# A two-layer decoder trunk on one core: early memsets and first fills on VectorE, routing tables made in two steps, the overflow path written as loops

## The chip, the core and the metric

The kernel runs on one core of a Trainium2 chip. Its time is what the device reports for one execution, in microseconds (us); of several runs the median is taken. PE is TensorE, DVE VectorE, ACT ScalarE, POOL GpSimd, and SP the engine that only issues transfers and waits. Each engine runs its own instructions in order; semaphores tie them together.

## What is computed

A sequence of 256 tokens of width 1024 passes two layers. Each sub-layer is `x + gate * fn(rms_norm(x) * (1 + scale) + shift)`, where shift, scale and gate come from the conditioning vector `c` by a 1024 x 3072 product:

```python
def ada_params(c, w, b):
    mod = jax.nn.silu(c) @ w + b
    shift, scale, gate = jnp.split(mod, 3, axis=-1)
...
    for i in range(DEPTH):
...
        x = modulated_residual(x, c, norm_g[i, 0], mod_w[i, 0], mod_b[i, 0], mixer)
        x = modulated_residual(x, c, norm_g[i, 1], mod_w[i, 1], mod_b[i, 1], channel)
    return rms_norm(x, final_g)
```

Layer 0 has a short gated convolution and a dense SwiGLU, layer 1 dilated attention and eight SwiGLU experts, of which each token takes two.

All weights are float32 in HBM, some 395 MB; every one of them is read once.

## The kernel before, in words

**The weight stream.** One object, `Stream`, holds all weight loads in the order of use. SP issues them (L279 for split weights, L305, L343 and L354 for the modulation weights, L480 for the experts) into a ring of buffers of 1 MB. A load is issued when its buffer is free. Each transfer counts on one of eight semaphores in turn, so SP also waits until the transfer eight places earlier has landed. For the dense layers a weight is split into two rounded halves: ACT writes `whi` (L218), DVE the rest `wlo` (L220), and PE multiplies three times (`hTh` by `whi`, `hTl` by `whi`, `hTh` by `wlo`).

**The start.** The first modulation (`Mod` 0) is summed on PE: `cb`, silu of `c` spread over 32 columns, times the raw weights, into `tp`. DVE adds the sums to the bias rows in `macc` (L317), PE spreads the rows with the selector tiles `pick`, and DVE multiplies with the norm weights `gb` (L374). `macc` is cleared by POOL before SP may issue the transfers of its bias rows; in SP's program these stand behind the first two weight loads and ahead of all others:

```python
            self.acc = pool.tile([P, 512], F32, name="macc", bufs=2)
            self.summed = False
            gp.memset(self.acc, 0.0)
            for n, c0 in enumerate(cols):
                dma.dma_start(self.acc[64 * n:64 * n + 1], self.b[c0:c0 + 512].rearrange("(o n) -> o n", o=1))
```

`gb` is one row copied to all partitions by POOL's `partition_broadcast`; `dif`, the table behind the identity `ident`, is a POOL `iota`.

**The dense feed-forward stage** takes 22 weight units, one after the other. `hooks` hangs other work behind units by their number; `make_routing` hangs behind unit 0. It makes the experts' tables: POOL iotas `part`, `slotc`, `tri`, `slot`, and nine DVE operations on them. In DVE's order it stands ahead of `hTl` of the second half of the features, which unit 2 is the first to need.

**The experts** run one after another, 34.6 MB of weights each. Ahead of expert 1 every engine that takes part reads the flag `over` from SBUF, which says whether an expert has over 128 tokens, and branches (L1514, L1515). With these inputs none has, so `overflow()` is not run. PE's first product of expert 1 waits for DVE to have passed that If.

Of the kernel before, what the change touches and what calls it, by code (L numbers as in the profile page):

```python
# [22 lines left out]
KT = D // P  # L23
FF = 2816
NE = 8
# [4 lines left out]
EPS = 1e-6  # L30
# [22 lines left out]
def trunk_kernel(ctx: ExitStack, tc: tile.TileContext, a, out):  # L53
    nc = tc.nc
    ve, sc, pe, gp = nc.vector, nc.scalar, nc.tensor, nc.gpsimd

    cst = ctx.enter_context(tc.tile_pool(name="cst", bufs=1))
    pers = ctx.enter_context(tc.tile_pool(name="pers", bufs=1))
# [4 lines left out]
    def f32(ap):  # L63
        return ap.bitcast(F32)
# [16 lines left out]
    x = pers.tile([P, NT, D], F32, name="x")  # L81
# [23 lines left out]

    pick = [early.tile([P, P], F32, name=f"pick{n}") for n in range(2)]
    for n in range(2):
        gp.memset(pick[n], 0.0)
        for r in (64 * n, 64 * n + 32):
            gp.memset(pick[n][r:r + 1], 1.0)  # L110
    warm = cst.tile([P, 1], F32, name="warm")
    sc.activation(warm, eps, AF.Sqrt)

# [29 lines left out]
    class Stream:  # L143
# [143 lines left out]
    class Mod:  # L287
# [5 lines left out]
        def start_pe(self, pool, cols, dma=gp):  # L293


            self.acc = pool.tile([P, 512], F32, name="macc", bufs=2)
# [89 lines left out]
    mods = [Mod(s) for s in range(4)]  # L386
# [293 lines left out]
    rw = cst.tile([P, KT, NE], F32, name="rw")  # L680
# [6 lines left out]
    slotc = cst.tile([P, 7], F32, name="slotc")  # L687
    slot = None

    def make_routing():  # L690
        nonlocal slot

        part = cst.tile([P, 7], I32, name="part")
        gp.iota(part, pattern=[[0, 7]], base=0, channel_multiplier=1)
        partf = cst.tile([P, 7], F32, name="partf")
        for c, n, m, base, step in ((0, 1, 63, 1, 0), (1, 2, 31, 65, 32), (3, 4, 31, 1, 32)):
            c = slice(c, c + n)
            ve.tensor_scalar(part[:, c], part[:, c], m, None, op0=OP.bitwise_and)
            gp.iota(slotc[:, c], pattern=[[step, n]], base=base, channel_multiplier=0, allow_small_or_imprecise_dtypes=True)
        ve.tensor_copy(partf, part)  # L700
        ve.tensor_add(slotc, slotc, partf)
        nc.sync.dma_start(rw, a["router_w"][0].rearrange("(k p) e -> p k e", p=P))
        gp.iota(tri, pattern=[[1, NE], [-1, NE]], base=0, channel_multiplier=0, allow_small_or_imprecise_dtypes=True)
# [551 lines left out]
    def overflow():  # L1255

        wg, wu, wd = a["moe_w_gate"][0], a["moe_w_up"][0], a["moe_w_down"][0]
        ov = moe.tile([P, FF], F32, name="ov", tag="acts")
        hs = ov[:, 2048:2560]
        wts = deque(pers.tile([P, 512], F32, name="ovw", tag="rtmp", bufs=3) for _ in range(2))  # L1260
        gov = moe.tile([P, NT, NE], F32, name="gov")
        po, pg = sums_of
        for i in range(NT):
            ve.scalar_tensor_tensor(gov[:, i], px[:, i], P + 0.5, gates[:, i], op0=OP.is_gt, op1=OP.mult)
        for i in range(NT):
            hTo = ov[:, :D].rearrange("p (k t) -> p k t", t=P)
            for q in range(2):
                c = slice(q * 512, q * 512 + 512)
                ve.tensor_add(hs, f32(hh[:, i, c]), f32(hl[:, i, c]))
                p = turn_tile().rearrange("p (k t) -> p k t", k=4)  # L1270
                for k in range(4):
                    pe.transpose(p[:, k], hs[:, k * P:(k + 1) * P], ident)
                sc.activation(hTo[:, 4 * q:4 * q + 4], p, AF.Copy)
            for e in range(NE):
                for f0 in range(0, FF, 256):
                    for n, w in enumerate((wg, wu)):
                        for k in range(0, KT, 2):
                            wts.rotate()
                            wt = wts[0].rearrange("p (k n) -> p k n", k=2)
                            gp.dma_start(wt, w[e, k * P:(k + 2) * P, f0:f0 + 256].rearrange("(k p) n -> p k n", p=P))  # L1280
                            for kk in range(2):
                                mm(pg[:, n * 512:n * 512 + 256], hTo[:, k + kk], wt[:, kk], k + kk == 0, k + kk == KT - 1)
                    sg = ov[:, D:D + 256]
                    sc.activation(sg, pg[:, :256], AF.Silu)
                    ve.tensor_mul(sg, sg, pg[:, 512:768])
# [3 lines left out]
                    sT = ov[:, D + 256:D + 512].rearrange("p (f t) -> p f t", t=P)  # L1289
                    sc.activation(sT.rearrange("p f t -> p (f t)"), p[:, :256], AF.Copy)  # L1290
                    for f in range(2):
                        r0 = f0 + f * P
                        for h in range(2):
                            wts.rotate()
                            wt = wts[0]
                            gp.dma_start(wt, wd[e, r0:r0 + P, h * 512:h * 512 + 512])
                            mm(po[:, h * 512:h * 512 + 512], sT[:, f], wt, r0 == 0, r0 + P == FF)
                for h in range(2):
                    c = slice(h * 512, h * 512 + 512)
                    og = ov[:, D + 512:D + 1024]  # L1300
                    ve.tensor_mul(og, po[:, c], mods[3].G[:, c])
                    ve.scalar_tensor_tensor(x[:, i, c], og, gov[:, i, e:e + 1], x[:, i, c], op0=OP.mult, op1=OP.add)

    hh = hl = None
    rs, nxt, lps = {}, {}, {}
# [199 lines left out]
                ve.scalar_tensor_tensor(x[:, i, cs], ps[i][c], gates[:, i, e:e + 1], x[:, i, cs], op0=OP.mult, op1=OP.add)  # L1505

    _, n_all = nc.values_load_multi_w_load_instructions(counts[0:1, :], engines=[mybir.EngineType.PE], min_val=0, max_val=S)
    engines = [mybir.EngineType.PE, mybir.EngineType.Activation, mybir.EngineType.DVE, mybir.EngineType.Pool]
    tc.mark_branch_hint_location("overflow", "LikelyTaken", engines)
    for e in range(NE):  # L1510
        pr, b = divmod(e, 2)
        n_before, n_of = n_of, n_all[e]
        if e == 1:
            flag = nc.values_load(over[0:1, 0:1], engines=engines, min_val=0, max_val=1)  # L1514
            with tc.If(flag > 0, label="overflow"):  # L1515
                overflow()
        if e == NE - 2:
            fg = pers.tile([P, D], F32, name="fg", tag="gb")
# [138 lines left out]
```

## Time and profile before

| | us |
|---|---|
| median of 3 runs | 1209.56 (1209.32 to 1211.14) |
| the profiled execution | 1213.32 |
| its span | 1211.5 |
| PE busy | 1106.7 (91%) |
| DVE busy | 548.5 (45%) |
| ACT busy | 320.7 (26%) |
| POOL busy | 32.1 (3%) |
| read from HBM | 395.45 MB, 327 GB/s over the span |

The stages by the clock of the trace: the convolution layer to about 150 us, the dense feed-forward layer to 380, attention to 490, the experts to the end. PE's busy share is an average over stages in which different things end last, so it says little about an edit in one of them. The stretch and the wait around each edit have to be read.

### The profile page before, as it was taken

The numbers are of one execution on the slowest core, as the hardware profiler recorded it, in microseconds if no ns is written. First come the engines' busy times: TensorE is split into PE (matmuls) and PEld (weight loads), VectorE is DVE, ScalarE is ACT, GpSimd is POOL, SyncE is SP. The second block draws the span as 40 slices with busy tenths as digits, with TensorE's granted clock in tenths as the row PEclk, the third lists the DMA queues.
The fourth block names the chain that finished last, engine by engine and source line by source line (L and its number), as shares of the span: only waits on it lengthen the run. The fifth ranks groups of instructions, "written<-read, shape, count | busy, mean of one in ns | idle before, by whom it ended". The sixth has DMA issues, their size and how long they took to land. (4 is left out here: it accounts for less than half of the span.)

```text
span 1211.5 us, 20568 instructions
## 1 busy us (share of the span) xinstructions
PE 1106.7 (91%) x8658; PEld 614.3 (51%) x8658; DVE 548.5 (45%) x853; ACT 320.7 (26%) x517; POOL 32.1 (3%) x56
## 2 busy tenths in 40 slices
PE   3999979999999999897999999999999999998985
PEld 0799679998878877432323333333333333322233
DVE  1599778897869966431222121211221222222123
ACT  2244434444344573321111110110010011110111
POOL 3010110000001000000000000000000000000000
PEclk9899989999999999998999999999999999999998
DMA  6898768787847835799999999999779999999993
GB/s 241 312 351 315 234 236 296 276 288 300 295 168 261 287 140 208 301 404 407 406 405 407 404 406 408 377 361 400 290 281 404 404 374 408 405 406 408 404 367 109
DMA packets 139401, 398.41 MB, mean 329 GB/s; under 512 B 11299, under 2 KB 22331, under 8 KB 139274
## 3 DMA queue, kind: packets, MB, share of 16 engines
q1 hardware_dynamic: 138698, 396.47, 86.1%
q8 instruction: 101, 1.65, 0.6%
q14 instruction: 26, 0.21, 0.0%
q0 software_dynamic: 576, 0.07, 0.0%
HBM read 395.45 MB, written 1.05 MB: 327 GB/s over the span
## 5 line engine op out<-in xcount | busy, mean ns | idle before, releaser
L73 PE MATMUL mm<-raw,xg 128*32 128x512 f32 (+1 forms) x1616 | 242.5, 566 | 21.4 <-DVEq L1515 7.6
L73 PE MATMUL mm<-rawr,xg 128*32 128x512 f32 (+1 forms) x1360 | 167.7, 559 | 7.7 <-PEq L1417 4.2
L220 DVE TENSOR_TENSOR wlo<-raw,whi 128x1024 fp32r<-128x1024 f32 (+2 forms) x130 | 154.0, 1222 | 30.8 <-ACT whi L218 30.0
L218 ACT ACTIVATE whi<-raw 128x1024 fp32r<-128x1024 f32 (+2 forms) x130 | 132.2, 1045 | 125.7 <-PE mm L73 90.7
L1424 DVE TENSOR_TENSOR gu<-gu,mm 64x512 f32<-64x512 f32 (+1 forms) x96 | 62.0, 646 | 217.7 <-ACT gu L1423 217.3
L73 PE MATMUL mm<-hTl,whi 128*128 128x256 f32 x544 | 148.8, 287 | 8.0 <-DVE hTl L531 8.0
L73 PE MATMUL mm<-hTh,whi 128*128 128x256 f32 x544 | 151.4, 293 | 1.4 <-ACT hTh L530 1.4
L73 PE MATMUL mm<-hTh,wlo 128*128 128x256 f32 x544 | 147.9, 285 | 0.8 <-DVE wlo L220 0.8
L73 PEld LDWEIGHTS mm<-raw,xg 128*32 128x32 f32 x1616 | 70.0, 111 | 131.8 <-issue 112.7
L1423 ACT ACTIVATE gu<-mm 64x512 f32<-64x512 f32 (+1 forms) x96 | 51.5, 552 | 304.6 <-PE mm L73 190.7
L73 PEld LDWEIGHTS mm<-hTl,whi 128*128 128x128 f32 x544 | 102.7, 195 | 11.3 <-DVE hTl L531 8.2
L73 PEld LDWEIGHTS mm<-hTh,whi 128*128 128x128 f32 x544 | 103.9, 198 | 3.9 <-ACT hTh L530 2.1
L73 PEld LDWEIGHTS mm<-rawr,xg 128*32 128x32 f32 x1360 | 51.1, 109 | 103.3 <-issue 89.3
L73 PEld LDWEIGHTS mm<-hTh,wlo 128*128 128x128 f32 x544 | 102.5, 194 | 1.0 <-DVE wlo L220 1.0
L73 PE MATMUL mm<-raw,acts 128*32 128x512 f32 (+1 forms) x784 | 87.8, 566 | 12.7 <-DMA raw<-in_moe_w_down_dram 6.9
L73 PE MATMUL mm<-rawr,acts 128*32 128x512 f32 x608 | 73.7, 595 | 4.4 <-PEq L1415 1.6
L1435 DVE COPY acts<-tp 128x256 f32<-128x256 f32 (+1 forms) x48 | 19.2, 401 | 92.5 <-ACT acts L1243 92.3
L73 PEld LDWEIGHTS mm<-raw,acts 128*32 128x32 f32 x784 | 26.4, 110 | 67.1 <-issue 53.6
L285 DVE SCALAR_TENSOR_TENSOR acc_ab<-raw,csil,acc_ab 128x1024 f32<-128x1024 f32 x40 | 51.2, 1281 | 6.4 <-DMA acc_ab<-in_mod_b_dram 5.7
L73 PE MATMUL mm<-whi,hTh 128*128 128x512 f32 (+1 forms) x128 | 50.1, 409 | 0.8 <-ACT hTh L530 0.7
L73 PE MATMUL mm<-rawx,xg 128*32 128x512 f32 (+1 forms) x224 | 47.9, 560 | 2.1 <-DMA rawx<-in_moe_w_up_dram 1.5
L1481 DVE TENSOR_TENSOR og<-mm,G 128x512 f32<-128x512 f32 x14 | 9.0, 686 | 89.4 <-PEq L1417 51.8
(267 smaller groups left out, 1331.2 us busy)
## 6 DMA issues: line engine op xcount, KB each, us to landing
raw<-in_moe_w_down_dram SPq DMA_DIRECT2D x36, 1024.0 KB, 13.1
rawr<-in_moe_w_down_dram SPq DMA_DIRECT2D x66, 512.0 KB, 10.0
raw<-in_mod_w_dram SPq DMA_DIRECT2D x64, 512.0 KB, 5.1
raw<-in_moe_w_gate_dram SPq DMA_DIRECT2D x29, 1024.0 KB, 14.0
raw<-in_moe_w_up_dram SPq DMA_DIRECT2D x27, 1024.0 KB, 12.1
rawr<-in_moe_w_up_dram SPq DMA_DIRECT2D x48, 512.0 KB, 10.2
rawr<-in_moe_w_gate_dram SPq DMA_DIRECT2D x48, 512.0 KB, 10.5
raw<-in_mod_w_dram SPq DMA_DIRECT2D x16, 1024.0 KB, 5.9
```

What stands on the lines that cost most here:

```text
L73: pe.matmul(o, l, r, start=start, stop=stop, skip_group_check=True)
L218: sc.activation(hi[:n, :c1 - c0], src, AF.Copy)
L220: ve.tensor_sub(lo_, src, f32(hi)))
L285: ve.scalar_tensor_tensor(acc, w, csil[:, k:k + 1], acc, op0=OP.mult, op1=OP.add)
L1423: sc.activation(a[64:, :N], bank[g][:64, :N], AF.Silu)
L1424: ve.tensor_mul(a[64 * g:64 * g + 64, :N], a[64:, :N], bank[g][64:, :N])
L1435: copy(acts[:, 8 * r:8 * r + 2 * nb, g:g + 32].rearrange("p (j m) t -> p m j t", j=2), v[:, :, n])
L1481: ve.tensor_mul(og[:, g - 1], bank[g], G2)
```

## The change

- POOL's memsets of `ones`, `eps`, `pick` and `macc` go to DVE. The first `macc` becomes a tile of its own name, `macc0`, cleared ahead of `cb`; `ones` and `ident` come behind `cb`.
- `make_routing` is cut in two. `start_routing` (behind unit 0) issues the load of the router's weights and the POOL iotas; `make_routing` (behind unit 13) does the DVE operations, now eight, and the `slot` iota.
- `overflow()` handles both halves of the tokens for one load of a weight, and loops over experts and blocks of 256 rows at run time. All five engines, SP among them, now read the flag and branch. The mark of the branch as likely taken is gone.

```diff
-    gp.memset(ones, 1.0)
     eps = cst.tile([P, 1], F32, name="eps")
-    gp.memset(eps, 4 * EPS)
-    ident = cst.tile([P, P], F32, name="ident")
-    ve.tensor_scalar(ident, dif, 0.0, None, op0=OP.is_equal)
+    ve.memset(eps, 4 * EPS)
+
+    pick = [early.tile([P, P], F32, name=f"pick{n}") for n in range(2)]
+    for n in range(2):
+        ve.memset(pick[n], 0.0)
+        for r in (64 * n, 64 * n + 32):
+            ve.memset(pick[n][r:r + 1], 1.0)
...
+    macc0 = early.tile([P, 512], F32, name="macc", bufs=2)
+    ve.memset(macc0, 0.0)
     ve.tensor_copy(cb, csil[:, :, None].to_broadcast([P, KT, 32]))
...
+    ve.memset(ones, 1.0)
+    ident = cst.tile([P, P], F32, name="ident")
+    ve.tensor_scalar(ident, dif, 0.0, None, op0=OP.is_equal)
...
-            gp.memset(self.acc, 0.0)
+            if dma is nc.sync:
+                self.acc = macc0
+            else:
+                self.acc = pool.tile([P, 512], F32, name="macc", bufs=2)
+                ve.memset(self.acc, 0.0)
...
+    def start_routing():
+        nc.sync.dma_start(rw, a["router_w"][0].rearrange("(k p) e -> p k e", p=P))
+        gp.iota(tri, pattern=[[1, NE], [-1, NE]], base=0, channel_multiplier=0, allow_small_or_imprecise_dtypes=True)
+
+        gp.iota(part, pattern=[[0, 7]], base=0, channel_multiplier=1)
...
-                 0: make_routing}
+                 0: start_routing, 13: make_routing}
...
+        with tc.For_i(0, NE) as e:
+            for t in po:
+                ve.memset(t, 0.0)
+            with tc.For_i(0, FF, 256) as f0:
...
-    engines = [mybir.EngineType.PE, mybir.EngineType.Activation, mybir.EngineType.DVE, mybir.EngineType.Pool]
-    tc.mark_branch_hint_location("overflow", "LikelyTaken", engines)
...
-            flag = nc.values_load(over[0:1, 0:1], engines=engines, min_val=0, max_val=1)
-            with tc.If(flag > 0, label="overflow"):
+            flag = nc.values_load(over[0:1, 0:1], min_val=0, max_val=1)
+            with tc.If(flag > 0):
```

How the rows stand. POOL's program at the start, before:

```order
L94 ISA
L94 IOTA dif 128x128
L96 MEMSET ones 128x128
L98 MEMSET eps 128x1
L108 MEMSET pick_88 128x128
L110 MEMSET pick_88 1x128 x2
L108 MEMSET pick_89 128x128
L110 MEMSET pick_89 1x128 x2
L298 MEMSET macc 128x512
L332 ISA
L332 ISA gb<-rows 128x1024
```

The memsets there have left POOL, which goes from `dif` straight to the broadcast. (An ISA row without operands sets POOL up for the operation behind it.) DVE's program at the start, after (L322 is what L317 was):

```order
L97 MEMSET eps 128x1
L101 MEMSET pick_81 128x128
L103 MEMSET pick_81 1x128 x2
L101 MEMSET pick_82 128x128
L103 MEMSET pick_82 1x128 x2
L108 MEMSET macc 128x512
L109 COPY cb<-csil 128x256
L110 MEMSET ones 128x128
L112 TENSOR_SCALAR ident<-dif 128x128
L322 TENSOR_TENSOR macc<-macc,tp 128x512
```

Nothing ahead of `ident` on DVE needs POOL any more; before, `ident` was the first row, and `cb` the second.

DVE's program in the first units of the feed-forward stage, before:

```order
L220 TENSOR_TENSOR wlo<-raw,whi 128x1024 x6
L698 TENSOR_SCALAR part<-part 128x1
L698 TENSOR_SCALAR part<-part 128x2
L698 TENSOR_SCALAR part<-part 128x4
L700 CAST partf<-part 128x7
L701 TENSOR_TENSOR slotc<-slotc,partf 128x7
L704 TENSOR_SCALAR tri<-tri 128x64
L705 TENSOR_SCALAR upper<-dif 128x128
L706 MEMSET ones_b 128x128
L707 CAST ident_b<-ident 128x128
L531 TENSOR_TENSOR hTl<-tp,hTh 128x4x128 x2
L285 SCALAR_TENSOR_TENSOR acc_g<-raw,csil,acc_g 128x1024 x2
```

and after:

```order
L222 TENSOR_TENSOR wlo<-raw,whi 128x1024 x6
L536 TENSOR_TENSOR hTl<-tp,hTh 128x4x128 x2
L287 SCALAR_TENSOR_TENSOR acc_g<-raw,csil,acc_g 128x1024 x2
L222 TENSOR_TENSOR wlo<-raw,whi 128x1024 x2
L287 SCALAR_TENSOR_TENSOR acc_g<-raw,csil,acc_g 128x1024 x2
```

`hTl` (now L536) follows `wlo` (now L222) at once; the rows from `part` to `ident_b` stand 13 units later.

SP's program at the If, before:

```order
L480 DMA rawm<-in_moe_w_up_dram 128x1024
L480 DMA raw<-in_moe_w_gate_dram 128x2x1024
L480 DMA raw<-in_moe_w_up_dram 128x2x1024
L1515 UNCONDITIONAL_BRANCH
L480 DMA raw<-in_moe_w_gate_dram 128x2x1024
L480 DMA rawx<-in_moe_w_up_dram 128x2x1024
L480 DMA rawr<-in_moe_w_gate_dram 128x1024
```

and after (L485 is what L480 was, a load of expert weights):

```order
L485 DMA rawh<-in_moe_w_up_dram 128x1024 x2
L485 DMA raw<-in_moe_w_gate_dram 128x2x1024
L485 DMA raw<-in_moe_w_up_dram 128x2x1024
L1530 TENSOR_LOAD over
L1530 ISA x2
L1531 COMPARE_AND_BRANCH
```

Before, SP read no flag; the branch of L1515 there has no condition. Now SP reads the flag, and the next load of weights stands behind its comparison.

## Rows read from the trace of the kernel before

**Rows 1.** The page, its parts 1 and 2: the whole span.

```profile
PE 1106.7 (91%) x8658; PEld 614.3 (51%) x8658; DVE 548.5 (45%) x853; ACT 320.7 (26%) x517; POOL 32.1 (3%) x56
...
DMA  6898768787847835799999999999779999999993
```

**Rows 2.** Busy time by stretch: us, busy of each engine, clock, DMA share, GB/s.

```profile
2.00:5.00 3.00, 0.00 (x0) 0.00 (x0) 0.00 (x0) 1.58 (x3) 0.00 (x0) 1.00 0.84 260
5.00:15.00 10.00, 1.93 (x8) 0.20 (x8) 0.52 (x2) 0.20 (x1) 2.20 (x10) 1.00 0.18 53
15.00:25.00 10.00, 7.29 (x24) 1.00 (x24) 0.09 (x1) 0.00 (x0) 6.59 (x8) 1.00 1.04 396
...
31.00:41.00 10.00, 8.75 (x38) 6.09 (x39) 7.42 (x9) 3.49 (x5) 0.00 (x0) 0.53 1.04 372
```

**Rows 3.** Timeline, first 20 us: start, duration, engine, line, [idle before it <- releaser].

```profile
1.18 0.93 SPq L305 DMA_DIRECT2D raw<-in_mod_w_dram  x2
2.40 0.21 ACT L102 ACTIVATE csil<-cin 128x8 f32<-128x8 f32 x1 [0.32 <-DMA cin<-in_c_dram]
...
9.18 0.24 POOL L94 IOTA dif<- 128x128 f32 x1 [8.74 <-issue]
...
9.59 0.38 DVE L104 COPY cb<-csil 128x256 f32<-128x256 f32 x1
...
11.16 0.53 POOL L298 MEMSET macc<- 128x512 f32 x1
11.71 0.59 SPq L300 DMA_DIRECT2D macc<-in_mod_b_dram  x2
...
17.50 1.30 POOL L332 PARTITION_BROADCAST gb<-rows  x1 [5.82 <-issue]
```

**Rows 4.** Timeline, 24 to 32 us.

```profile
24.91 0.69 DVE L317 TENSOR_TENSOR macc<-macc,tp 128x512 f32<-128x512 f32 x1 [14.94 <-DMA x<-in_x_dram]
25.20 0.63 ACT L503 ACTIVATE scr<-x 128x512 f32<-128x512 f32 x1 [15.35 <-DMA x<-in_x_dram]
...
28.50 0.68 DVE L374 SCALAR_TENSOR_TENSOR rows<-tp,gb 128x512 f32<-128x512 f32 x1
...
30.46 0.68 DVE L737 TENSOR_TENSOR h<-h,rows 128x512 f32<-128x512 f32 x1
```

**Rows 5.** Timeline, 157 to 172 us, around the routing tables.

```profile
156.59 4.45 DVE L220 TENSOR_TENSOR wlo<-raw,whi 128x1024 fp32r<-128x1024 f32 x3
...
168.34 0.14 POOL L694 IOTA part<- 128x7 int32 x1 [9.38 <-issue]
...
168.52 0.30 DVE L698 TENSOR_SCALAR part<-part 128x1 int32<-128x1 int32 x3 [7.48 <-POOL part L694]
...
169.67 1.27 DVE L531 TENSOR_TENSOR hTl<-tp,hTh 128x512 fp32r<-128x512 f32 x2
...
171.00 0.58 PE L73 MATMUL mm<-hTl,whi 128*128 128x256 f32 x1 [7.98 <-DVE hTl L531]
```

**Rows 6.** Busy time by stretch, the dense feed-forward stage.

```profile
171.00:177.00 6.00, 6.00 (x28) 6.00 (x29) 5.93 (x6) 0.91 (x1) 0.00 (x0) 0.50 0.39 126
...
180.00:240.00 60.00, 60.00 (x493) 59.04 (x492) 49.39 (x58) 28.39 (x30) 1.67 (x2) 1.00 0.85 300
240.00:300.00 60.00, 59.12 (x460) 57.34 (x459) 51.33 (x61) 27.60 (x30) 0.00 (x0) 1.00 0.79 282
```

**Rows 7.** Line 1403, a memset of the third accumulator's size on DVE.

```profile
L1403 DVE MEMSET tp<- x2: 485/485/485, 500.7 to 501.2; 128x512 f32 x2
```

**Rows 8.** Timeline of DVE where the last `macc` memset will stand.

```profile
131.52 2.36 DVE L220 TENSOR_TENSOR wlo<-raw,whi 128x1024 fp32r<-128x1024 f32 x2 [3.63 <-ACT whi L218]
```

**Rows 9.** The line of the overflow flag's If, per sequencer: min/median/max ns, first and last start.

```profile
L1515 PEldq COMPARE_BRANCH  x1: 1682/1682/1682, 564.2 to 564.2; - x1
```

**Rows 10.** Busy time by stretch, around that If.

```profile
562.00:571.00 9.00, 1.44 (x19) 0.32 (x12) 4.64 (x7) 2.35 (x4) 0.00 (x0) 0.73 1.03 406
```

**Rows 11.** Loads issued in 575 to 600 us: count, KB, median us to landing.

```profile
rawr<-in_moe_w_up_dram SPq DMA_DIRECT2D x3, 512.0 KB, 10.2
```

More of the change, by code (lines that the diff above doesn't have):

```diff
@@ L103, in trunk_kernel @@
     cb = early.tile([P, KT, 32], F32, name="cb")
+    macc0 = early.tile([P, 512], F32, name="macc", bufs=2)
+    ve.memset(macc0, 0.0)
     ve.tensor_copy(cb, csil[:, :, None].to_broadcast([P, KT, 32]))
[L106 to L110, printed above, removed]
+    ve.memset(ones, 1.0)
+    ident = cst.tile([P, P], F32, name="ident")
+    ve.tensor_scalar(ident, dif, 0.0, None, op0=OP.is_equal)
     warm = cst.tile([P, 1], F32, name="warm")
@@ L293, in start_pe @@
         def start_pe(self, pool, cols, dma=gp):
-            self.acc = pool.tile([P, 512], F32, name="macc", bufs=2)
             self.summed = False
-            gp.memset(self.acc, 0.0)
+            if dma is nc.sync:
[3 more added lines that the diff above has]
+                ve.memset(self.acc, 0.0)
             for n, c0 in enumerate(cols):
@@ L688, in trunk_kernel @@
     slot = None
+    part = cst.tile([P, 7], I32, name="part")
+    def start_routing():
+        nc.sync.dma_start(rw, a["router_w"][0].rearrange("(k p) e -> p k e", p=P))
+        gp.iota(tri, pattern=[[1, NE], [-1, NE]], base=0, channel_multiplier=0, allow_small_or_imprecise_dtypes=True)
+        gp.iota(part, pattern=[[0, 7]], base=0, channel_multiplier=1)
+        for c, n, base, step in ((0, 1, 1, 0), (1, 2, 65, 32), (3, 4, 1, 32)):
+            gp.iota(slotc[:, c:c + n], pattern=[[step, n]], base=base, channel_multiplier=0,
+                    allow_small_or_imprecise_dtypes=True)
     def make_routing():
         nonlocal slot
-        part = cst.tile([P, 7], I32, name="part")
-        gp.iota(part, pattern=[[0, 7]], base=0, channel_multiplier=1)
         partf = cst.tile([P, 7], F32, name="partf")
-        for c, n, m, base, step in ((0, 1, 63, 1, 0), (1, 2, 31, 65, 32), (3, 4, 31, 1, 32)):
-            c = slice(c, c + n)
+        for c, m in ((slice(0, 1), 63), (slice(1, 7), 31)):
             ve.tensor_scalar(part[:, c], part[:, c], m, None, op0=OP.bitwise_and)
-            gp.iota(slotc[:, c], pattern=[[step, n]], base=base, channel_multiplier=0, allow_small_or_imprecise_dtypes=True)
         ve.tensor_copy(partf, part)
         ve.tensor_add(slotc, slotc, partf)
-        nc.sync.dma_start(rw, a["router_w"][0].rearrange("(k p) e -> p k e", p=P))
-        gp.iota(tri, pattern=[[1, NE], [-1, NE]], base=0, channel_multiplier=0, allow_small_or_imprecise_dtypes=True)
         ve.tensor_scalar(tri, tri, 0.0, None, op0=OP.is_gt)
@@ L1258, in overflow @@
         ov = moe.tile([P, FF], F32, name="ov", tag="acts")
-        hs = ov[:, 2048:2560]
+        hTo = ov[:, :2048].rearrange("p (i k t) -> p i k t", i=NT, t=P)
+        sg, sT = ov[:, 2048:2304], ov[:, 2304:2560].rearrange("p (f t) -> p f t", t=P)
         wts = deque(pers.tile([P, 512], F32, name="ovw", tag="rtmp", bufs=3) for _ in range(2))
-        gov = moe.tile([P, NT, NE], F32, name="gov")
-        po, pg = sums_of
+        og = pers.tile([P, 512], F32, name="ovo", tag="rtmp", bufs=3)
@@ L1263, in overflow, with load @@
+        gov = moe.tile([P, 2, NT, NE], F32, name="gov")
+        po, pg = sums_of, rest
+        def load(src):
+            wts.rotate()
+            dst = wts[0].rearrange("p (k n) -> p k n", k=2) if src.shape[1] > P else wts[0]
+            gp.dma_start(dst, src.rearrange("o (k p) n -> p (o k) n" if src.shape[1] > P else "o p n -> p (o n)", p=P))
+            return wts[0]
         for i in range(NT):
-            ve.scalar_tensor_tensor(gov[:, i], px[:, i], P + 0.5, gates[:, i], op0=OP.is_gt, op1=OP.mult)
@@ L1265, in overflow @@
-        for i in range(NT):
-            hTo = ov[:, :D].rearrange("p (k t) -> p k t", t=P)
+            ve.scalar_tensor_tensor(gov[:, 0, i], px[:, i], P + 0.5, gates[:, i], op0=OP.is_gt, op1=OP.mult)
             for q in range(2):
                 c = slice(q * 512, q * 512 + 512)
-                ve.tensor_add(hs, f32(hh[:, i, c]), f32(hl[:, i, c]))
+                ve.tensor_add(og, f32(hh[:, i, c]), f32(hl[:, i, c]))
                 p = turn_tile().rearrange("p (k t) -> p k t", k=4)
                 for k in range(4):
[L1272 to L1280, printed above, removed]
-                            for kk in range(2):
[L1282 to L1285, printed above, removed]
@@ new lines, in overflow @@
+                    pe.transpose(p[:, k], og[:, k * P:(k + 1) * P], ident)
+                sc.activation(hTo[:, i, 4 * q:4 * q + 4], p, AF.Copy)
+        with tc.For_i(0, NE) as e:
+            for t in po:
+                ve.memset(t, 0.0)
+            with tc.For_i(0, FF, 256) as f0:
+                for n, w in enumerate((wg, wu)):
+                    for k in range(0, KT, 2):
+                        wt = load(w[bass.ds(e, 1), k * P:(k + 2) * P, bass.ds(f0, 256)])
+                        for i in range(NT):
+                            for kk in range(2):
+                                o = pg[:, i * 512 + n * 256:i * 512 + n * 256 + 256]
+                                mm(o, hTo[:, i, k + kk], wt[:, kk * 256:kk * 256 + 256], (n, k, kk) == (0, 0, 0),
+                                   k + kk == KT - 1)
+                for i in range(NT):
+                    sc.activation(sg, pg[:, i * 512:i * 512 + 256], AF.Silu)
+                    ve.tensor_mul(sg, sg, pg[:, i * 512 + 256:i * 512 + 512])
@@ L1288, in overflow @@
                         pe.transpose(p[:, f * P:(f + 1) * P], sg[:, f * P:(f + 1) * P], ident)
-                    sT = ov[:, D + 256:D + 512].rearrange("p (f t) -> p f t", t=P)
-                    sc.activation(sT.rearrange("p f t -> p (f t)"), p[:, :256], AF.Copy)
+                    sc.activation(sT, p[:, :256].rearrange("p (f t) -> p f t", t=P), AF.Copy)
                     for f in range(2):
-                        r0 = f0 + f * P
                         for h in range(2):
[L1294 to L1297, printed above, removed]
+                            wt = load(wd[bass.ds(e, 1), bass.ds(f0 + f * P, P), h * 512:h * 512 + 512])
+                            mm(po[i][:, h * 512:h * 512 + 512], sT[:, f], wt, False, False)
+            for i in range(NT):
                 for h in range(2):
                     c = slice(h * 512, h * 512 + 512)
-                    og = ov[:, D + 512:D + 1024]
-                    ve.tensor_mul(og, po[:, c], mods[3].G[:, c])
-                    ve.scalar_tensor_tensor(x[:, i, c], og, gov[:, i, e:e + 1], x[:, i, c], op0=OP.mult, op1=OP.add)
+                    ve.tensor_mul(og, po[i][:, c], mods[3].G[:, c])
+                    ve.scalar_tensor_tensor(x[:, i, c], og, gov[:, 0, i, 0:1], x[:, i, c], op0=OP.mult, op1=OP.add)
+            ve.tensor_copy(gov[:, 1], gov[:, 0])
+            ve.tensor_copy(gov[:, 0, :, :NE - 1], gov[:, 1, :, 1:])
     hh = hl = None
```

## The prediction

> **What bounds the kernel now.** I began with the page [rows 1]. PE is busy 91% of the span, but busy shares add up stages that end on different things, and the second row there shows it: the transfers run at 6 to 9 tenths in the first half and at 9 in nearly all of the second. So the edits have to be costed one by one, each in its own stretch.
>
> The first stretch, by the view of busy time in stretches [rows 2]: from 15 to 25 us the transfers fill their engines (396 GB/s, share 1.04), from 2 to 5 us they nearly do, and between 5 and 15 us they move 53 GB/s. The start is bound by the stream of weights, and the stream stands still in its middle. The timeline of the same stretch says why [rows 3]. SP issues two weight loads at 1.18 us and nothing more until 11.71. What it waits for is the memset of `macc` on POOL, 11.16 + 0.53 = 11.69. POOL is that late because its first `iota` begins only at 9.18, after 8.74 us in which it waited for nothing that the profile names. DVE's `cb`, which the first products need, is just as late (9.59), though its input was there at 2.40 + 0.21 = 2.61: `ident` stands ahead of it and needs that `iota`.
>
> The second stretch is the beginning of the dense feed-forward stage [rows 5], which comes after the chain of the first norm [rows 4]. POOL takes 9.38 us between its last broadcast and the iota `part`. DVE, in order, stands 7.48 us for it, with `hTl` queued behind, and PE stands 7.98 us for `hTl`. From there to the end of the stage PE is the bound: 60.00 us of 60 from 180 to 240 [rows 6], with DVE at 49.39.
>
> The experts are bound by the stream (1.03 in [rows 10]).
>
> **Part 1, the start.** After the change, SP needs DVE's memsets only. I cost them by their sizes: the 128x512 one at 0.49 [rows 7], two of 128x128 at up to 0.38 (the row of `cb`, which is larger), four single rows and `eps` at some 0.2 each (nine small operations of DVE took 169.67 - 168.52 = 1.15 in [rows 5], 0.13 each, and here some wait for the one before), in sum 0.5 + 0.8 + 1.0 = 2.3. DVE has nothing else to do there. POOL's idle time begins at 9.18 - 8.74 = 0.4; from about then on the memsets end near 3.0, and `cb` near 3.4. The third load then goes out at 3.0 and not at 11.71: 8.7 us earlier. The stream gives the same: in 10 us from 5 to 15 it moved 0.53 MB, which takes 0.53/0.396 = 1.3 us at the rate of the next row, so 8.7 us of it were lost [rows 2]. It is then the stream that sets when the sums in `macc` are complete (24.91) and when `x` is there (25.20), both in [rows 4], so both come 8.7 us earlier, near 16.3.
>
> What is late next? The norm weights `gb`, which DVE needs at 28.50 - 8.7 = 19.8. POOL still starts its iota at 9.18; behind it comes the broadcast, which took 5.82 us from when POOL was free to its start and 1.30 to run [rows 3]: 9.4 + 5.8 + 1.3 = 16.5. If it took the 9.38 of [rows 5] instead, `gb` would be there at 20.1, and 0.3 us would be lost. I take nothing.
>
> The second `macc` is now cleared on DVE, 0.49 us, just ahead of the addition at 30.46 which the first transposes on PE wait for; there DVE has no gap, so I charge 0.5. The third stands ahead of a `wlo` that waits 3.63 us for ACT [rows 8]; it is hidden there, and costs 0.5 if that wait goes. Sum of part 1: 8.7 - 0.5 = 8.2 us.
>
> **Part 2, the routing tables.** The nine DVE operations leave the place ahead of `hTl`. DVE ends `wlo` at 156.59 + 4.45 = 161.04, so `hTl` can begin 8.6 us earlier than 169.67 and its first half is there at about 161.7. PE reached the point where it needs it at 171.00 - 7.98 = 163.02. So the whole 7.98 us go, with over 1 us to spare.
>
> More goes with them. After the pause PE ran at half clock (0.50, that is 1.2 GHz) from 171 to 177 us: 28 products in 6 us, where 60 us at full clock held 493 [rows 6]. At that pace 28 take 3.4 us, so 2.6 us were lost. The row of the clock itself would say 3.0 (6 us at half). I take 2.6. Without a pause the clock has no reason to fall here; in the whole of the next 120 us, with PE busy, it is 1.00. Sum of part 2: 8.0 + 2.6 = 10.6 us.
>
> Does PE then run into something else? From 180 to 240 us DVE is busy 49.39 us while PE is busy 60.00, a reserve of 18%, and the transfers have a share of 0.85 [rows 6]. I take nothing; the bound is that PE gains only what DVE was kept standing, 7.48 us and none of the clock.
>
> The eight operations now stand behind unit 13, in a stretch with PE at 59.12 of 60 and DVE at 51.33. The nine together took 1.15 us. They lie beside PE's work: 0, at most 1.2. The router's load and the iotas of POOL stay behind unit 0; POOL will be as late with them as now, but the next that asks is unit 13. That is twelve units of 48 products at 60/493 us, some 70 us on.
>
> What POOL does in those idle times is described in the Trainium skill, page "GPSIMD Engine Reference", section "2.1 Instruction dispatch": the first call to a freshly loaded kernel waits about 6 us (5.95 measured) for its code, without a visible instruction. The rows agree in kind (a configuration, then 5.82, 8.74 and 9.38 us without one), not in size for the iotas. By the page's figure the pause in part 2 would be 3.4 us shorter and my sum 15.4; the rows are of this kernel, and they decide.
>
> **Part 3, the overflow path.** It isn't run. What is run is the flag's load and branch, now on SP too. On PE the branch took 1.68 us [rows 9], and PE was busy only 1.44 of the 9 us around it, since it waited for DVE to pass. Through those 9 us the stream still moved 406 GB/s [rows 10], because SP had loads under way. A load issued there takes 10.2 us to land [rows 11], so up to eight transfers stand in the queue when SP stops to read the flag. If SP pays what PE paid, some 2 us, the queue does not run dry: 0. The bound above is 2 us. PE's wait for DVE stays, for the overflow path still writes `x` on DVE; since the stream bounds this stage, a microsecond more or less in it is worth nothing. A smaller program brings nothing that a row shows.
>
> **Sum.** 8.2 + 10.6 = 18.8 us. Both are early, and between them and the experts PE is the bound, so the shift should reach the end. The working is made on the profiled execution (1213.32 us, span 1211.5); it ran 3.8 us above the median, and I take the gain off the median: 1209.56 - 18.8 = **1190.8 us**.
>
> **The rivals.**
> - *Only part 2 pays.* The start could be held by something that comes at its old time: `gb`, if POOL's code loads take longer now that the stream runs beside them, or DVE's first memsets, if they start late. For it: POOL's waits differ (5.82 to 9.38), and the start will have more transfers beside them. Against: `gb` has 3.3 us to spare. In full it would give 1209.56 - 10.6 = 1199.0. Chance 0.12.
> - *Only part 1 pays.* The pause on PE is filled by another wait, because DVE and ACT gained a lead in it. Against: DVE itself was standing. 1209.56 - 8.2 = 1201.4. Chance 0.11.
> - *More than both.* The clock is low at the start too, 0.53 on the mean from 31 to 41 us with PE busy 8.75 us [rows 2]. Without the gap in the products ahead of it, it may not fall; that would be worth up to 8.75 x 0.47 = 4.1 us more: 1186.7. Chance 0.06.
> - *Slower, through SP.* SP is the one queue that must never stand, and it now reads a flag in the midst of the experts. It decides when SP stands longer than the queue lasts plus the gain, 10.2 + 18.8 = 29 us; at 40 us the time would be 1209.56 - 18.8 + 30 = 1221. For it: SP's next load stands behind the branch. Against: what the flag waits for (`over`) was written before expert 0, and the dearest of the branches seen took 1.68 us. Chance 0.05.
> - *It doesn't do what it says*: POOL's late start holds DVE all the same, and another POOL result holds `hTl`. The rows of the new order show neither. No change, 1209.6. Chance 0.04.
>
> The slower rival has a page behind it: the Trainium skill, "Runtime: NRT & Kernel Launch", section "Instruction fetch mechanics", says that a taken branch to a place outside the small window of fetched code must first fetch it. PE's 1.68 us agrees with that; by that rule SP pays once, about as much.
>
> **How the numbers follow.** My forecast has 0.62. The range runs from the lowest case (1186.7, and 0.5 for the memset that I charged) to the first rival (1199.0, and 1 us for the bounds of parts 2 and 3): 1186 to 1200. It leaves out the second rival, the slower one and no change, 0.20 together. A measurement of this kernel can tell about 0.2% (2.4 us) from no change. Faster by more than that: 0.62 + 0.12 + 0.11 + 0.06 = 0.91. Within: 0.04. Slower: 0.05.
>
> **What would show it.** Part 1: SP's bias transfers at about 3 us, no idle stretch of the transfers between 5 and 15, the sums in `macc` near 16, `gb` ready before DVE asks. Part 2: no idle time of PE ahead of `hTl`, a clock of 1.00 through that unit, POOL's 9.4 us still there with nobody waiting. Part 3: the stream at 406 GB/s through the If, SP's branch near 2 us. The prediction is wrong if `gb` or a POOL result becomes the wait in the start, if PE stands for `wlo` in units 2 to 5, or if the transfers show a hole where SP reads the flag.

## The result, and the profile after

The kernel after takes 1190.13 us (median of 4 runs, 1189.3 to 1192.88), the kernel before 1210.35 beside it (4 runs, 1209.32 to 1212.58). The ratio is 0.9834 with a 95% interval of 0.9812 to 0.9857: 20 us less, 17 to 23. The forecast was 1190.8. The experiments will show that the total came out right though two of its three terms were off, in opposite directions.

The page of the kernel after, parts 1 and 2:

```profile
PE 1102.9 (93%) x8658; PEld 614.1 (52%) x8658; DVE 549.9 (46%) x863; ACT 320.3 (27%) x517; POOL 29.6 (2%) x45
...
DMA  9888797887937915999999999999779999999994
```

PE's share rose from 91% to 93% with the same number of products. The transfers' first slice, 6 tenths in [rows 1], is at 9.

Busy time by stretch of the kernel after, columns as in [rows 2]:

```profile
2.00:5.00 3.00, 0.00 (x0) 0.03 (x1) 1.04 (x5) 1.83 (x4) 0.00 (x0) 1.00 0.86 255
5.00:15.00 10.00, 7.54 (x25) 1.08 (x26) 0.23 (x1) 0.00 (x0) 0.24 (x1) 1.00 1.03 367
15.00:25.00 10.00, 4.43 (x16) 1.25 (x14) 5.98 (x17) 6.07 (x14) 2.82 (x4) 1.00 1.05 382
25.00:31.00 6.00, 5.08 (x24) 4.40 (x28) 4.79 (x7) 2.65 (x4) 4.09 (x5) 0.51 1.01 367
```

From 5 to 15 us the transfers now move 367 GB/s at a share of 1.03, where they moved 53. The half clock of the start is still there (0.51 from 25 to 31 us), only earlier.

The timeline of the kernel after, its first 24 us (start, duration, engine, line, idle time before and what ended it):

```profile
2.49 0.48 DVE L108 MEMSET macc<- 128x512 f32 x1 [0.15 <-issue]
...
3.00 0.59 SPq L305 DMA_DIRECT2D macc<-in_mod_b_dram  x2
...
5.00 4.07 PE L73 MATMUL tp<-raw,cb 128*32 128x512 f32 x10 [5.00 <-DMA raw<-in_mod_w_dram]
...
9.25 0.24 POOL L94 IOTA dif<- 128x128 f32 x1 [8.69 <-issue]
...
17.14 0.69 DVE L322 TENSOR_TENSOR macc<-macc,tp 128x512 f32<-128x512 f32 x1 [7.39 <-PE tp L73]
17.27 0.63 ACT L508 ACTIVATE scr<-x 128x512 f32<-128x512 f32 x1 [13.06 <-DMA x<-in_x_dram]
...
18.63 1.30 POOL L337 PARTITION_BROADCAST gb<-rows  x1 [9.14 <-DMA x<-in_x_dram]
...
20.57 0.68 DVE L379 SCALAR_TENSOR_TENSOR rows<-tp,gb 128x512 f32<-128x512 f32 x1
...
22.67 0.48 DVE L303 MEMSET macc<- 128x512 f32 x1
23.08 0.63 DVE L746 TENSOR_TENSOR h<-h,rows 128x512 f32<-128x512 f32 x1
...
23.76 0.66 PE L541 MATMUL tp<-ident,h 128*128 128x128 f32 x4 [3.90 <-DVE h L746]
```

SP's bias transfers go out at 3.00 and not at 11.71 [rows 3], 8.7 us earlier, as worked out. POOL's iota is as late as ever (9.25), with nobody but `ident` waiting. The sums in `macc` (17.14) and `x` (17.27) come 7.8 and 7.9 us earlier than in [rows 4], the `h` addition (23.08) 7.4 us earlier. The clearing of the second `macc` at 22.67 stands on the path, for 0.4 us (22.67 to 23.08). `gb` is complete at 18.63 + 1.30 = 19.93, and DVE asks for it at 20.57: 0.6 us of slack, not 3.3.

The timeline at the beginning of the feed-forward stage of the kernel after, DVE and then POOL:

```profile
145.23 7.85 DVE L222 TENSOR_TENSOR wlo<-raw,whi 128x1024 fp32r<-128x1024 f32 x6
153.01 1.27 DVE L536 TENSOR_TENSOR hTl<-tp,hTh 128x512 fp32r<-128x512 f32 x2
```

```profile
160.50 0.23 POOL L699 IOTA tri<- 128x64 f32 x1 [9.49 <-issue]
```

`hTl` follows `wlo` at once. In the kernel before, 8.63 us lay between the end of `wlo` and `hTl` [rows 5]. POOL still takes 9.49 us from its broadcast to its iota, and nobody waits for it. Busy time by stretch there:

```profile
150.00:153.00 3.00, 3.00 (x28) 3.00 (x27) 3.00 (x2) 1.28 (x2) 1.01 (x1) 1.00 1.02 397
153.00:180.00 27.00, 27.00 (x228) 27.00 (x227) 24.59 (x25) 12.72 (x13) 1.11 (x7) 1.00 0.92 332
180.00:240.00 60.00, 60.00 (x493) 59.04 (x492) 52.66 (x81) 26.75 (x29) 1.95 (x3) 1.00 0.82 291
```

PE has no idle time and a clock of 1.00, where [rows 5, 6] had 7.98 us of waiting and 6 us at 0.50.

The If of the flag in the kernel after, two of its sequencers (min/median/max ns), and then the stretch ahead of SP's branch and the one with it:

```profile
L1531 PEldq COMPARE_BRANCH  x1: 1783/1783/1783, 545.1 to 545.1; - x1
...
L1531 SPq COMPARE_BRANCH  x1: 50/50/50, 570.5 to 570.5; - x1
```

```profile
562.00:570.00 8.00, 7.84 (x65) 2.83 (x68) 2.73 (x4) 0.00 (x0) 0.00 (x0) 1.00 1.02 404
570.00:574.00 4.00, 3.68 (x40) 1.17 (x36) 1.53 (x3) 1.66 (x3) 0.00 (x0) 1.00 1.03 412
```

PE pays 1783 ns for its branch, SP 50. SP's load of the flag begins at 569.6 and its branch ends near 570.6, so it loses 1 us, and the stream keeps 404 GB/s ahead of it and 412 with it and behind it.

### The profile page after: what moved, and what is told of

Its sections match the earlier page's. It is cut to its first block, busy times and chain, and to the rows that moved or that the text cites. A ratio compares the mean times of both kernels' runs of the same rounds, so it can differ in the third digit from the quotient of the medians.

```text
span 1188.1 us, 20567 instructions
## 1 busy us (share of the span) xinstructions
PE 1102.9 (93%) x8658; PEld 614.1 (52%) x8658; DVE 549.9 (46%) x863; ACT 320.3 (27%) x517; POOL 29.6 (2%) x45
## 3 DMA queue, kind: packets, MB, share of 16 engines
q8 instruction: 101, 1.65, 0.6%
## 5 line engine op out<-in xcount | busy, mean ns | idle before, releaser
L73 PE MATMUL mm<-raw,xg 128*32 128x512 f32 (+1 forms) x1616 | 245.8, 570 | 19.1 <-DVEq L1531 7.1
L222 DVE TENSOR_TENSOR wlo<-raw,whi 128x1024 fp32r<-128x1024 f32 (+2 forms) x130 | 153.8, 1221 | 27.5 <-ACT whi L220 26.6
## 6 DMA issues: line engine op xcount, KB each, us to landing
rawr<-in_moe_w_up_dram SPq DMA_DIRECT2D x48, 512.0 KB, 10.4
```

The source lines that it names most:

```text
L222: ve.tensor_sub(lo_, src, f32(hi)))
```

## The experiments

The gains in us below are the ratio's distance from 1, times the median of the kernel before in the same set of runs (1209.91, 1209.1 and 1210.28 us).

**Part 1 alone.** The lines of the start from the change, all else as before.

> The kernel before with part 1 alone (memsets and first macc on DVE, cb ahead of ident). Theory: the gain of the start adds to that of part 2, so some 7.5 us here (the h addition came 7.4 us earlier in the kernel after): 0.9938 of before. The pause of PE at the feed-forward stage stays: hTl waits 7 to 8 us, the row mask of that stage comes 7.4 us earlier and not more. Rival (the pause swallows the lead, because POOL's iotas there end at a fixed time): POOL's broadcast ahead of them is itself early, so I expect no loss; if the rival holds, the lead is gone at hTl and the time is that of before.

1202.24 us, ratio 0.9943 (0.9924 to 0.9961): a gain of 6.9 us (4.7 to 9.2). The rival fell: the lead is not lost; in this execution it was worth 7.0 us at the `h` addition. The theory was wrong on the pause: PE waits 4.81 us ahead of `hTl` and not 7.98. Of these 3.2 us less, 2.05 come from POOL, which stood 7.33 us between broadcast and iota and not 9.38. (The prediction takes this time for a load of code, and I call it POOL's load. In the kernels before and after, no packet of an instruction queue moves in it, so the trace doesn't show what POOL does there.) The row of `gb` is new (timeline of this kernel, POOL and DVE):

```profile
19.56 1.30 POOL L337 PARTITION_BROADCAST gb<-rows  x1 [10.14 <-issue]
...
20.90 0.69 DVE L379 SCALAR_TENSOR_TENSOR rows<-tp,gb 128x512 f32<-128x512 f32 x1 [0.50 <-POOL gb L337]
```

POOL took 10.14 us to the broadcast, and DVE now waits for `gb`, 0.50 us. In the kernel after it took 9.14, and this wait is not there.

**The first `macc` alone.**

```diff
+    macc0 = early.tile([P, 512], F32, name="macc", bufs=2)
+    ve.memset(macc0, 0.0)
     ident = cst.tile([P, P], F32, name="ident")
```

> The kernel before, with only the first macc cleared on DVE as the first thing; cb stays behind ident, all else on POOL. Theory: the stream moves on at about 2 us, but the products start at about 10 us with cb; 32 products at 0.30 us follow, so the sums are there near 19.9 and not 24.9: some 5 us of gain at the first h addition. Rival (the stream alone sets the start): the full 7.5 us. Rival (cb alone does): 0.

1203.26 us, ratio 0.9941 (0.9919 to 0.9964): 7.1 us, as much as all of part 1. My 5 us were wrong and the rival, the stream alone, was right. Products still begin at 10.13, but they had been slow only because they waited for transfers. With the weights at hand 24 of them take 4.87 us (busy time by stretch of this kernel):

```profile
5.00:15.00 10.00, 4.87 (x24) 1.19 (x25) 0.52 (x2) 0.20 (x1) 1.67 (x9) 1.00 1.03 373
```

So PE caught up, and the sums were there at 16.60. Here too DVE then waited for `gb`, 1.06 us.

**`cb` alone.**

```diff
-    ident = cst.tile([P, P], F32, name="ident")
-    ve.tensor_scalar(ident, dif, 0.0, None, op0=OP.is_equal)
...
     ve.tensor_copy(cb, csil[:, :, None].to_broadcast([P, KT, 32]))
+    ident = cst.tile([P, P], F32, name="ident")
+    ve.tensor_scalar(ident, dif, 0.0, None, op0=OP.is_equal)
```

> The kernel before, with only cb moved ahead of ident on DVE; macc is still cleared by POOL at 11.2. Theory: PE starts its products near 5 us but the loads behind the bias rows still go out at 11.7, so the sums in macc stay near 24.9 and x near 25.2: 0. Rival (the late products hold the start): the sums come several us earlier.

One run, 1210.75 us: no gain. PE's first product came at 5.64 and the sums at 25.02, as before. So one memset that SP waits for was all of part 1, as far as these times can tell (4.4 to 9.8 us for the memset alone).

**Part 2 alone.** `start_routing` behind unit 0, `make_routing` behind unit 13, all else as before.

> The kernel before with part 2 alone (tables made in two steps). Theory: the pause of 7.98 us and the half clock behind it go, 10.6 us together: 0.9912 of before. Rival a (the clock costs nothing, only the pause counts): 8.0 us, 0.9934. Rival b (without part 1 the pause goes into a wait for transfers): under 5 us, and a wait of PE for a weight's transfer or for DVE wlo in units 2 to 6.

1201.77 us, ratio 0.9937 (0.9914 to 0.9959): 7.6 us (5.0 to 10.4). In the profile the pause and the half clock are gone, and the row mask of the stage (the first DVE operation on the tile `mask`, L670 in the kernel before) comes 11.6 us earlier than in the profiled execution before (182.85 against 194.45). The time alone doesn't tell rival a (8.0) from the theory (10.6); rival b fell, since PE has no wait in the units that follow.

**The iotas early, the DVE work in its old place.**

```diff
+    def early_iotas():
+        gp.iota(part, pattern=[[0, 7]], base=0, channel_multiplier=1)
...
             m0.start_pe(pool, (0, D), nc.sync)
+            early_iotas()
             m0.start_rows(nc.sync)
```

> The kernel before, with the POOL iotas part, slotc and tri issued in the first 20 us, ahead of the first broadcast; the DVE operations and the slot iota stay behind unit 0 of the feed-forward stage. Theory: what held PE is POOL's 9.4 us between broadcast and iota and not the DVE work, so the pause goes all but about 0.1 us although nine DVE operations still stand ahead of hTl: 10 us, 0.9917 of before, as much as part 2 alone. Rival (the nine operations, or the load of the router's weights, hold hTl): no gain, and idle time of PE ahead of hTl remains above 1 us.

1202.08 us, ratio 0.9936 (0.9914 to 0.9958): 7.7 us, the same as part 2. The timeline of this kernel, DVE and PE around `hTl`:

```profile
160.83 0.28 DVE L705 TENSOR_SCALAR part<-part 128x1 int32<-128x1 int32 x3
...
161.89 1.28 DVE L531 TENSOR_TENSOR hTl<-tp,hTh 128x512 fp32r<-128x512 f32 x2
...
163.22 0.39 PE L73 MATMUL mm<-hTl,whi 128*128 128x256 f32 x1 [0.35 <-DVE hTl L531]
```

The DVE operations take 161.89 - 160.83 = 1.06 us ahead of `hTl`, and PE waits 0.35. So it was POOL's lateness that held PE, and not the tables' work.

**More products in the pause.** 56 of the kind of the unit, behind its first product.

```diff
+            if fill and (kk, f, p) == (0, 0, 1):
+                spare = mm_tile()
+                for _ in range(fill):
+                    mm(spare[:, :256], w, xT[0][:, k0 + kk], True, True)
```

> The kernel before, with 56 more products (of the same kind, their result not used) on PE in the pause ahead of hTl: some 6.8 us of the 7.98. Theory: the pause stays and ends at the same time, but the clock stays at 1.00 behind it, so 2.6 us of the 10.6 come back (171 to 177 us at full clock). Rival (the clock falls for another reason, or what is won runs into DVE): 0, and 0.50 in the records behind the pause. A loss would show if the extra products end behind hTl.

1205.86 us, ratio 0.9974 (0.9956 to 0.9991): 3.1 us. Busy time by stretch, in the pause and behind it:

```profile
163.00:170.00 7.00, 6.16 (x52) 5.95 (x50) 1.94 (x11) 0.29 (x1) 1.40 (x8) 1.00 0.27 109
170.40:176.40 6.00, 5.99 (x50) 5.99 (x51) 5.93 (x6) 1.24 (x2) 0.00 (x0) 1.00 0.38 114
```

The clock stays at 1.00, and 6 us hold 50 products where they held 28 [rows 6]. From the first product with `hTl` to the row mask it is 20.81 us (170.41 to 191.22) and was 23.45 (171.00 to 194.45): 2.64 us, the 2.6 of the prediction. In the kernel with the early iotas, which has no half clock here, the same way takes 20.82 us (163.22 to 184.04). The time doesn't show these 2.6 us: the added products also move PE's code, and moving it as far without running them gave 4.1 us by itself (below). So the clock's share stands on the profiles.

**Part 3 alone.** The new `overflow()` and its If, all else as before.

> The kernel before with part 3 alone (overflow path as loops, all five engines read the flag, no mark of likely taken). Theory: SP loses about 1 us, the queue of loads covers it: 0, within 2.4 us. Rival (the shorter program helps by fewer fetches of code, or the branch not marked costs): over 2.4 us to either side, and then the distance to before would step at the If or grow behind it.

1206.37 us, ratio 0.9973 (0.9958 to 0.9988): 3.3 us (1.5 to 5.1) for a path that isn't run. My 0 was wrong. No step shows at the If. In this execution two things were shorter. One is the pause ahead of `hTl` (timeline, POOL and PE):

```profile
165.00 0.14 POOL L694 IOTA part<- 128x7 int32 x1 [7.83 <-issue]
...
167.65 0.58 PE L73 MATMUL mm<-hTl,whi 128*128 128x256 f32 x1 [5.31 <-DVE hTl L531]
```

POOL's load took 7.83 us and the pause 5.31. The new path is not needed for that: the kernel of part 1, with the old path, had a short pause too. The other lies at the end, and it led to the next four runs.

**Parts 1 and 2 without part 3.**

> The kernel after with the overflow path and the If of before: parts 1 and 2 without part 3. Theory (part 3 is worth the pause of PE that the programs with the old path show some 20 us from the end): 1 to 3 us slower than the kernel after, with an idle stretch of PE of 1.0 to 2.7 us that no event ends, in the last column block of expert 7. Rival (part 3 is worth nothing, and the 3.3 us measured for it alone are scatter): as the kernel after, and no such idle stretch.

1194.71 us, ratio 0.9866 (0.984 to 0.9891): 16.2 us (13.2 to 19.4), 3.9 less than the whole change; the two intervals overlap. The idle stretch is there. PE's timeline of this kernel, 20 us from the end, and then the same place in the kernel before and in the kernel after:

```profile
1168.63 1.46 PE L73 MATMUL mm<-raw,acts 128*32 128x256 f32 x19
1173.04 1.25 PE L73 MATMUL mm<-raw,acts 128*32 128x256 f32 x13 [2.95 <-issue]
```

```profile
1184.84 3.52 PE L73 MATMUL mm<-raw,acts 128*32 128x256 f32 x43
1191.03 1.93 PE L73 MATMUL mm<-raw,acts 128*32 128x256 f32 x13 [2.66 <-issue]
```

```profile
1166.14 1.92 PE L73 MATMUL mm<-raw,acts 128*32 128x256 f32 x24 [0.15 <-PEq L1433]
1168.21 1.93 PE L73 MATMUL mm<-raw,acts 128*32 128x256 f32 x32 [0.15 <-PEq L1433]
```

Each is the block of 24 and then 32 products of the last expert's down projection (one row can hold several). After 19 of the 32 PE stands 2.95 and 2.66 us, for nothing that an event shows; in the kernel after it runs them through. All seven programs with the old path and no added PE instructions have this pause at this product: 1.03, 1.31, 1.84, 2.66, 2.66, 2.66 and 2.95 us. None of the other seven has it there.

What this costs goes beyond the pause. Busy time by stretch behind it, in the kernel before and then in the kernel of part 2 alone, whose pause was 1.84 us:

```profile
1191.03:1195.03 4.00, 3.85 (x22) 1.95 (x26) 0.26 (x1) 0.00 (x0) 0.00 (x0) 0.60 0.02 4
```

```profile
1178.65:1182.65 4.00, 3.85 (x49) 2.19 (x49) 0.91 (x2) 0.51 (x2) 0.00 (x0) 1.00 0.01 4
```

Behind the four pauses of 2.66 us and more the granted clock was 0.56 to 0.60 on the mean of some 4 us, behind the three shorter ones 1.00. The last norm's sum on DVE, before and then after, gives the whole of it:

```profile
1204.01 0.16 DVE L1614 TENSOR_REDUCE v<-sums 128x2 f32<-128x6 f32 x1 [0.64 <-ACT scr L1585]
```

```profile
1180.57 0.16 DVE L1630 TENSOR_REDUCE v<-sums 128x2 f32<-128x6 f32 x1 [0.64 <-ACT scr L1601]
```

From the first of the 24 products to this sum it is 19.17 us before (1184.84 to 1204.01) and 14.43 after (1166.14 to 1180.57): 4.74 us. Over the seven programs with the pause it is 1.6 to 5.0 us more than 14.43, 3.6 on the mean. That is the size of the 3.3 and 3.9 us that part 3 was worth by time.

What arrives in that time shows in the view of the transfers, before, from 1188 to 1189 us (packets, MB, share):

```profile
q8 instruction: 1, 0.02, 6.8%
```

and in part 3 of its page for the whole span:

```profile
q8 instruction: 101, 1.65, 0.6%
```

One packet of 0.02 MB of the instruction queue lands within the pause. There are 101 in the span, 1.65 / 101 = 0.016 MB each, over the same 16 DMA engines as the weights. In each of the seven PE goes on 1.3 to 1.5 us after such a packet has landed (before: it moves from 1188.44 to 1189.54, and PE goes on at 1191.03). So the later the packet, the longer the pause. That it carries PE's code, the next runs show.

**16 and 56 transposes more in the branch that isn't run.** Both in the kernel before.

```diff
                     pe.transpose(p[:, k], hs[:, k * P:(k + 1) * P], ident)
+                if (i, q) == (0, 0):
+                    for _ in range(16):
+                        pe.transpose(p[:, 3], hs[:, 3 * P:4 * P], ident)
```

> The kernel before with 16 more transposes in the overflow branch, which is not run: the work done is the same, only PE's code behind the branch lies 16 products (32 instructions by pairs of load and product) further on. Theory (the pause near the end is a fetch of code at a fixed address): the pause stays, but comes 16 products earlier, after 3 products of its block of 32 and not after 19. Rival (the pause belongs to the data or to the end of the stream): it stays at the same product.

1207.14 us, ratio 0.9969 (0.9955 to 0.9983): 3.8 us faster through instructions that are never executed. PE's timeline:

```profile
1183.29 1.92 PE L73 MATMUL mm<-raw,acts 128*32 128x256 f32 x24
1185.36 0.59 PE L73 MATMUL mm<-raw,acts 128*32 128x256 f32 x3
1186.44 1.92 PE L73 MATMUL mm<-raw,acts 128*32 128x256 f32 x29 [0.49 <-issue]
```

The pause comes after 3 products of the 32 and not after 19: 16 earlier, as expected of code at a fixed address. Its length fell to 0.49 us, which I had not expected. The view of its transfers from 1183 to 1184 us says why:

```profile
q8 instruction: 1, 0.02, 7.0%
```

The code packet began here over 2 us ahead of the product that needs it (1186.44), and not within the pause; its landing at 1185.10 is 1.34 us ahead of that product, as in the seven. What sets when a packet begins is open.

> The kernel before with 56 more transposes in the overflow branch, which is not run, as many as the kernel with products in the pause ran. Theory (address of the code): the pause near the end is gone from its place, since the boundary then falls where PE waits for transfers anyway; 1 to 3 us faster than before. Rival (the 56 products that were run did it by their time): the pause is there as in the kernel before, same time.

1206.36 us, ratio 0.9966 (0.9952 to 0.9981): 4.1 us, no pause at that place, as expected. The kernel with products in the pause moved the code as far, and its time (3.1 us) needs no more than that.

**The pause brought back in the kernel after.**

> The kernel after with 52 transposes in the overflow branch, which is not run; PE's program is then 7680 instructions (30 times 256) shorter than before, and not 7784. Theory (address of the code, boundaries at a power of two of instructions up to 512): the pause of 1.0 to 2.7 us comes back at the same product as in the kernel before, and the time is 1 to 3 us above the kernel after. Rival (the new path cures the pause by its loops, or boundaries lie otherwise): no pause, same time as the kernel after.

1190.95 us, ratio 0.9844 (0.9822 to 0.9866), and no pause at that product. PE's timeline of this kernel, the block that follows it:

```profile
1171.49 2.38 PE L73 MATMUL mm<-raw,acts 128*32 128x256 f32 x32
```

These 32 products take 1.93 us elsewhere. The 0.45 us more are a stop behind the first of them, 18 products on from the place that I had expected, and PE goes on 1.4 us after a code packet has landed. So a program with the new path has such stops too, at another product: its loops don't cure them, and the path moves them. The sum over 7680 instructions fell. It rested on the Trainium skill, "Runtime: NRT & Kernel Launch", section "Instruction fetch mechanics", which says that code is refilled in blocks of 16 KiB, 256 instructions, and that the cost of crossing into the next is mostly hidden. The packets' size agrees; that it is hidden didn't hold in the seven programs above; and the place of a boundary did not come out of a count of the program's instructions as I made it.

**A version that might beat both.** The kernel after with 7 more products (128x512) on PE ahead of the first transposes, and the second `macc` cleared at the start.

> The kernel after, with 7 more products on PE (128x512, result not used) in its wait of 3.9 us ahead of the first transposes, and with the second macc cleared in the first 5 us. Theory: the first transposes start at full clock and 0.4 us earlier; but the first products with wlo wait for DVE anyway (32.3 us), so of the up to 4 us that the clock costs between 24 and 32 us only 0.5 to 1.5 come through: within 2.4 us of the kernel after by time, seen in the profile alone. Rival (the clock at the start is worth its full share): 3 to 4 us faster than the kernel after.

1190.27 us, ratio 0.9834 (0.9814 to 0.9854): no gain over the kernel after. Busy time by stretch, and PE's timeline:

```profile
24.00:34.00 10.00, 9.26 (x66) 7.14 (x65) 6.17 (x7) 2.98 (x4) 1.54 (x3) 1.00 1.02 356
```

```profile
19.42 6.17 PE L73 MATMUL mm<-macc,pick 128*128 128x512 f32 x14
25.43 1.04 PE L545 MATMUL tp<-ident,h 128*128 128x128 f32 x8
```

The clock no longer falls (1.00, against 0.51 from 25 to 31 us). But the 7 products (two records each) took 6.17 us, more than the wait of 3.9, so the transposes came 1.7 us later (25.43). The row mask of the feed-forward stage still came 0.8 us earlier (174.78 against 175.56): from the first transposes to it, 149.35 us and not 151.80. So the time shows no gain, but what the clock at the start is worth isn't measured: some 2.4 us came back, and the late transposes took 1.7 of them. The rival with 3 to 4 us is not decided.

## Why the prediction was right, and where it was not

**Part 1** (8.2) was right in its mechanism; at the first transposes it measured 7.4 us, and 6.9 (4.7 to 9.2) by time. The step "so both come 8.7 us earlier, near 16.3" was 0.8 too large: the stream ran at 367 GB/s and not at the 396 that I carried over. The memset's 0.4 to 0.5 was right. "`gb` has 3.3 us to spare" was wrong in size: POOL's load grew from 5.8 to 9.1 us once the stream ran beside it, and 0.6 us were left. The first rival was near: in the kernel of part 1 it cost 0.5 us, and 1.06 in the one with the first `macc` alone.

**Part 2** (10.6) was right in its mechanism. Each half has its experiment: the pause goes with the iotas alone, and the clock's 2.6 us measured 2.64 in the profile. By time it was worth 7.6 (5.0 to 10.4). The step that was off is the size: the term was taken from one execution (1213.32 us) and subtracted from the median (1209.56), and the pause is not the same in all. Among the profiled ones it was 7.98, 7.98, 8.37 and 8.41 us, but also 4.81, 5.31 and 5.82. In these three POOL's load was shorter (7.3 to 8.3 us). With what the half clock cost behind it (the way from the first product with `hTl` to the row mask, less 20.82) these seven lost 6.1 to 10.8 us, 9.2 on the mean. That the timed runs spread in the same way is likely, not shown, for they have no trace.

**Part 3** (0) failed at the step "A smaller program brings nothing that a row shows". A row did show it: PE's 2.66 us "issue" near the end of the trace before, where the stream no longer bounds the time and I had not looked. Part 3 is worth 3.3 us alone (1.5 to 5.1), and 3.9 on top of the others. The pause and the half clock behind it account for it: 1.6 to 5.0 us in seven traces, 3.6 on the mean. That the place of the code can bring this is shown by the 16 and the 56 transposes. That the new path does it in the same way is what the traces leave: in the four kernels with it the pause is gone from its product, and one of them has a shorter stop 18 products on. What was said of SP held in the main: it lost 1 us, hidden by its queue. Its branch took 0.05 us, and not the 1.68 of PE that the prediction carried over to it. The rival *Slower, through SP* fell.

The sum: 16.2 for parts 1 and 2 where I had 18.8, and 3.9 where I had 0. Together 20.1, against the 18.8 forecast. That the forecast time came within 1 us is in part luck: one term was too large and another missing. The two profiled executions fit the terms, each with its own size: at the row mask the kernel after is 18.9 us ahead (175.56 against 194.45), near the 18.8 of the two terms, and the end adds 4.7; the spans differ by 23.4.

## What to carry to other kernels

Ask of every engine that only issues transfers what it waits for: here one memset of half a microsecond, queued behind another engine's slow start, held the whole stream for 9 us. A wait for POOL between operations of different kinds is best met by issuing its work long before it is asked for. Read the trace to its last row: near the end, where no transfer bounds the time, the address of the code cost 1.6 to 5.0 us here, and a difference of that size between two versions need not come from what they compute.

## What the runs showed of the hardware

POOL's load ahead of its first broadcast lengthened with the traffic beside it. Busy time by stretch, from when POOL was free to the broadcast, before and then after:

```profile
11.69:17.50 5.81, 1.03 (x5) 0.18 (x2) 0.00 (x0) 0.00 (x0) 0.00 (x0) 1.00 0.63 214
```

```profile
9.49:18.63 9.14, 6.02 (x24) 1.22 (x25) 0.91 (x2) 1.33 (x4) 0.00 (x1) 1.00 1.03 387
```

5.81 us beside 214 GB/s, 9.14 beside 387. Of the other kernels, those with the old start had 5.80 to 6.08, the one with the early iotas 7.20 beside 278, and the five with the early stream 8.24 to 10.14 beside 393 to 398. So the two groups lie apart, but within the second the traffic does not order them. Ahead of the iota of the feed-forward stage the five executions of fourteen in which PE's clock had fallen in the layer ahead (0.89 on the mean from 138 to 154 us) had 7.1 to 8.3 us, the nine with 1.00 had 8.9 to 10.0. What ties the two is open.

A wait of PE of the same length does not always bring the clock down: the one of 2.3 us at the third `macc` was followed by full clock in nine executions and by a stretch at half clock in five.
